# Weights times values in fp32 on two column tiles, and the gate function in three late ScalarE steps

## The chip, the core and the metric

The kernel runs on one core of a Trainium2 chip. The metric is device time in microseconds (us) of one execution, median of several. The engines are named as in the profile: PE (TensorE, matmul), PEld (its weight loads), DVE (VectorE), ACT (ScalarE), POOL (GpSimd), SP (SyncE, here only DMA issue).

## What is computed

A hybrid decoder trunk of two layers on x of 1024 rows by 1024 columns, all in float32. The first layer is differential attention (8 heads of two score maps each). From its output one shared K and V is projected. The second layer is stick-breaking attention with 16 heads of width 64. Each layer's mixer output is multiplied by a SiLU gate before the output projection and the residual add. The part that the change touches, from the reference:

```python
def _stick_breaking(q, k, v):
    ...
        z = jnp.einsum('bhqd,bshd->bhqs', qb, k).astype(jnp.float32) * scale
        log_beta = jax.nn.log_sigmoid(z)
        log_1mb = jnp.where(mask, jax.nn.log_sigmoid(-z), 0.0)
        suffix = lax.cumsum(log_1mb, axis=3, reverse=True) - log_1mb
        a = jnp.where(mask, jnp.exp(log_beta + suffix), 0.0)
        return jnp.einsum('bhqs,bshe->bhqe', a.astype(v.dtype), v)
...
    o = o.reshape(b, s, SB_W) * jax.nn.silu(g)
    return x + o @ w_out
```

## The kernel before

PE's fp32 work is mostly done as three products in a type of lower precision (fp32r): each operand is split into a high part (rounded) and a low part (the rest), and high*high, high*low and low*high are summed in PSUM. The high part is an ACT copy out of PSUM, the low part a DVE subtraction. So a projection block (`group`, lines 192 to 194) is 24 matmuls of 512 or 256 columns.

A layer (`run_layer`) works through head pairs. For the second layer a pair `p` has two heads `c` of 64 columns each. While the attention of one pair runs ("main"), the projections of the next pair (K, V, then Q and gate) are merged in between as "fill" by estimated costs (`merge`); after the last pair the fill is the output projection. The final order on each engine is set by a scheduler from those costs and from priorities: `hp()` raises the priority of what stands in it. Queues are in order: an instruction that waits holds up all behind it on its engine.

Attention of a pair goes over four groups `m` of 256 query rows, each in two steps `s_step` (128 rows, both heads) and then steps `t_step`:

- `s_step` (`unit_s_b`): scores on PE (line 235; the two heads use the upper and the lower 64 rows of the array), a copy of the scores from PSUM by ACT (line 778), a causal mask on POOL (line 780), then the stick-breaking chain: sign bit by DVE (787), Exp and Ln by ACT (788, 789), a min-and-subtract by DVE (790), a scan by DVE (792), Exp by ACT (793).
- `t_step(c, t)` (`unit_t_b`): one head `c` and 256 keys. `transposed` makes up to four 128x128 transposes on PE (line 263), the high part `th` by ACT (269) and the low part `tl` by DVE (270); the last step of a group leaves one block out and has it filled with zeros by POOL (267, 268). Then four fp32r matmuls of 256 columns (808, 809) add to PSUM tile `av`: the weights are a 128x128 tile that holds the high part of V in 64 columns and the low part in the other 64. At the end of a group ACT copies one half of `av` (814) and DVE adds the other (815).

A group `m` has `m`+1 such steps a head, so a pair has 20, and the layer has 160, with 640 matmuls of lines 808 and 809. The tiles of V are made by `v_done`: two ACT copies and two DVE subtractions for each half (752, 753).

The gate (`silu`, both layers, 16 calls each): ACT copies the projection from PSUM to `g` (210), DVE sets the sign bit (211), ACT does Exp and Ln (212, 213), DVE min-and-subtract (214), ACT Exp (215), POOL the product with `g` (216).

Of the kernel before, what the change touches and what calls it, by code (L numbers as in the profile page):

```python
# [24 lines left out]
HALF = 512  # L25
# [6 lines left out]
def f32(ap):  # L32
    return ap.bitcast(F32)


def build(tc, ins, out):
    nc = tc.nc
    act, dve, pool, pe = nc.scalar, nc.vector, nc.gpsimd, nc.tensor
# [4 lines left out]

    mk = lambda name, bufs, **kw: ctx.enter_context(tc.tile_pool(name=name, bufs=bufs, **kw))
    B = {"proj": 2, "sc": 2, "tr": 3, "av": 1, "th": 3, "g2k": 3, "o": 6, "w": 8, "raw": 3, "ta": 1, "g1k": 2, "hpr": 1, "small": 12, "qk": 2, "hpe": -1, "hpw": -1,
         "al": 6, "bl": 7, "tb": 3, "oa": 0, "la": 0, "lb": 8, "lt": 0, "lead": 1.0, "leada": 0.02, "leadb": 0.02, "leadxa": 0.15, "leadxb": 0.1, "holda": 0, "holdb": 0, "c2": 1, "gca": 0, "gcb": 0, "prea": 2, "preb": 1, "warm": 16, "wp": 2, "hpx": -1, "nx": 1, "nk": 6, "hpo": 0, "ob": 2}
# [8 lines left out]
    layer_pool = lctx.enter_context(tc.tile_pool(name="la", bufs=1))  # L55
    def hp(k="hpe"):
        return tc.high_priority(offset=None if B[k] < 0 else B[k])

    act.preload_act_table_set("natural_log_exp_and_others")

# [33 lines left out]
    ident = C("ident", [P, P])  # L94
# [10 lines left out]
    warm = PS("tr", B["tr"])  # L105
# [100 lines left out]
    def silu(pg, u):  # L206

        g = g2k()
        with hp():
            act.activation(g, pg, AF.Copy)  # L210
        dve.tensor_scalar(u.bitcast(I32), g.bitcast(I32), -0x80000000, None, ALU.bitwise_or)
        act.activation(u, u, AF.Exp)
        act.activation(u, u, AF.Ln, bias=1.0)
        dve.scalar_tensor_tensor(u, g, 0.0, u, ALU.min, ALU.subtract)
        act.activation(u, u, AF.Exp)
        pool.tensor_tensor(u, g, u, ALU.mult)

    def chunks(n):
        if n <= 512:
# [3 lines left out]
    HI = (slice(0, 64), slice(64, 128))  # L223
# [29 lines left out]
    def transposed(ae, ao, t, last):  # L253


        pt = PS("tr", B["tr"])
        order = (1, 0) if last else (0, 1)
        skip = P if last else 0
        for i, b in enumerate(order):
            for j, a in enumerate((ae, ao)):  # L260
                o = (i * 2 + j) * P
                if o >= skip:
                    pe.transpose(pt[:, o:o + P], a[:, (2 * t + b) * P:(2 * t + b + 1) * P], ident)  # L263
        th = T("th", [P, HALF], B["th"], F32R)
        tl = T("tl", [P, HALF], B["th"], F32R)
# [69 lines left out]

    def alloc_kv(hd):
        if hd.v is None:
            hd.v = [T("v", [P, 4, 2, P], 4, F32R) for _ in range(2)]
            hd.k = (T("kh", [P, S], 2, F32R), T("kl", [P, S], 2, F32R))

    def alloc_q(hd, hf):
# [355 lines left out]
    for j in range(2):  # L697
        g = gq16[:, j, :]
# [33 lines left out]
    def qkv_b(p):  # L732
        hd = heads_b[p]

        def q_done(hf, pt):
            with hp():
                split_q(alloc_q(hd, hf), pt, SCALE)

        def k_done(hf, pt):
            alloc_kv(hd)  # L740
            sl = slice(hf * HALF, (hf + 1) * HALF)
            with hp():
                split_k(hd.k, sl, pt, None)

        def v_done(hf, pt):
            tr = v_rows(pt)
            t3 = tr.rearrange("p (r j e) -> p r j e", r=4, j=2)
            for j in range(2):
                hi = hd.v[hf][:, :, j, 64 * j:64 * j + 64]
                lo = hd.v[hf][:, :, j, 64 - 64 * j:128 - 64 * j]  # L750
                with hp():
                    act.activation(hi, t3[:, :, j, :], AF.Copy)
                    dve.tensor_tensor(lo, t3[:, :, j, :], f32(hi), ALU.subtract)

        def proj(done):
            return lambda W, hf: proj_t(W, xT2, hf, lambda pt: done(hf, pt))

        return [(lambda: w_pair(w_kv[p], cols[:, 16:24]), [proj(k_done), proj(v_done)]),
                (lambda: w_pair(w_b[p], cols[:, 8:16]), [proj(q_done)])]

    def unit_s_b(p, m):
        hd = heads_b[p]

        def s_step(qb):
# [3 lines left out]
            n = (qb + 1) * P  # L768
# [6 lines left out]
            def evac(off, w, n, pt):  # L775
                for t, cs in zip(z, heads):
                    t3 = t[:, :w2].rearrange("p (c n) -> p c n", c=len(cs))
                    act.activation(t3[:, :, off:off + w], pt[:, cs[0]:cs[-1] + 1, :w], AF.Copy)  # L778
                    if off + w == n:
                        pool.affine_select(t3[:, :, n - P:], t3[:, :, n - P:], [[0, len(cs)], [-1, P]], ALU.is_ge, -BIG,  # L780
                                           base=-1, channel_multiplier=1)

            scores(hd.q[qb // 4], hd.k, qb, evac)
            for t in z:
                zc = t[:, :w2]
                u = u4k()[:, :w2]
# [11 lines left out]
    def unit_t_b(p, m):  # L798
        hd = heads_b[p]
        box = {}  # L800

        def t_step(c, t):
            if c == 0 and t == 0:
                box["p"] = PS("av", B["av"])
            pc = box["p"][:, c * 256:c * 256 + 256]
# [4 lines left out]
            if t == m:  # L810
                hi = slice(64 * c, 64 * c + 64)
                lo = slice(64 - 64 * c, 128 - 64 * c)
                oc = hd.o[m // 2][hi, (m % 2) * 256:(m % 2) * 256 + 256]
                act.activation(oc, pc[lo, :], AF.Copy)
                dve.tensor_tensor(oc, pc[hi, :], oc, ALU.add)
                if c == 1:
                    hd.done[m // 2] += 1

        return [(4 * 55 + 4 * 109, lambda c=c, t=t: t_step(c, t)) for c in range(2) for t in range(m + 1)]

    def sink_b(rb, t, cs):
        nc.sync.dma_start(out[0, rb * P:(rb + 1) * P, cs[0]:cs[1]], t[:, cs[0]:cs[1]])
# [56 lines left out]
```

## Time and profile before

| | us |
|---|---|
| median of 3 runs (1469.36 to 1471.21) | 1470.85 |
| the profiled execution | 1470.77 |
| its span (first to last instruction) | 1469.0 |
| PE busy in the span | 1414.9 |
| DVE busy | 1088.0 |
| ACT busy | 943.5 |
| POOL busy | 288.2 |

A matmul's time in the profile reaches from its start to the end of its results, and the next one begins earlier, so the price of a matmul in a stream is the distance between two starts, not its duration. In the table of stretches below, each row gives a stretch (from:to in us, then its length), and for each engine the busy time in it and the number of instructions, then the mean granted clock of PE (1.00 is 2.4 GHz; the other level, 1.2 GHz, counts 0.5). The first layer and its output projection reach to about 690 us; the attention of the second layer, from its first weights times values, to about 1410.

### The profile page before, as it was taken

The page shows a single profiled execution, that of the slowest core. Times are in us where ns is not written, and L with a number is a line of the kernel's source. Part 1 is how long each engine was busy: PE and PEld are TensorE (multiplying, and loading weights), DVE is VectorE, ACT ScalarE, POOL GpSimd, SP SyncE. Part 2 cuts the span into 40 slices and gives each one's busy share as a digit, 9 for nine tenths or more (in the row PEclk, how much of TensorE's full clock was granted, in tenths as well). Part 3 has the DMA queues.
Part 4 walks back from the last instruction along what each step waited for, and adds up shares of the span by engine and source line. Part 5 has one row for each costly group of instructions (what it writes and reads, how often), then busy time and mean ns, then how long its engine had stood idle before and what let it go on. Part 6 is the DMA issues. An engine that isn't in the chain of part 4 may idle for free.

```text
span 1469.0 us, 24503 instructions
## 1 busy us (share of the span) xinstructions
PE 1414.9 (96%) x8944; PEld 1192.0 (81%) x8944; DVE 1088.0 (74%) x2251; ACT 943.5 (64%) x1940; POOL 288.2 (20%) x545
## 2 busy tenths in 40 slices
PE   8999999999999999999999998998989999988899
PEld 7888888888888888799877776777867777767699
DVE  7586777777776867875458786887878788889952
ACT  7555566656565655453468777787777887788720
POOL 0111212121212112100011321322333242323100
PEclk9999999999999999999999998999999999998899
DMA  5111111111111124623111110111101010233412
GB/s 202 58 30 44 44 44 44 44 44 44 44 44 44 44 72 173 215 94 108 58 58 30 35 53 29 51 37 44 43 8 51 30 58 29 91 111 125 177 72 80
DMA packets 43113, 99.40 MB, mean 68 GB/s; under 512 B 4848, under 2 KB 6640, under 8 KB 41968
## 3 DMA queue, kind: packets, MB, share of 16 engines
q1 hardware_dynamic: 42992, 97.83, 19.4%
q8 instruction: 71, 1.16, 0.3%
q14 instruction: 50, 0.41, 0.1%
HBM read 74.74 MB, written 23.07 MB: 67 GB/s over the span
## 4 chain that ended last, share of the span: by engine, by line
PE 76%; DVE 12%; ACT 5%; issue 4%; DMA 1%; POOL 0%; SPq 0%; ACTq 0%; DVEq 0%; POOLq 0%
PE proj L192 18%; PE proj L193 18%; PE proj L194 17%; PE sc L235 8%; PE tr L263 5%; DVE u4k L792 5%; DVE u4k L790 2%; PE av L808 2%; PE av L809 2%; DVE tl L270 1%; PE av L638 1%; PE av L640 1%; PE av L639 1%; ACT u4k L788 1%; PE tr L571 1%
## 5 line engine op out<-in xcount | busy, mean ns | idle before, releaser
L192 PE MATMUL proj<-ah,w 128*128 128x512 f32 x768 | 310.3, 404 | 4.1 <-DVE kl L243 4.1
L193 PE MATMUL proj<-al,w 128*128 128x512 f32 x768 | 309.8, 403 | 0.0
L194 PE MATMUL proj<-ah,w 128*128 128x512 f32 x768 | 308.9, 402 | 0.0
L192 PE MATMUL proj<-w,ah 128*128 128x256 f32 x992 | 289.8, 292 | 4.0 <-DVE v L422 1.9
L194 PE MATMUL proj<-w,al 128*128 128x256 f32 x992 | 285.0, 287 | 0.0
L193 PE MATMUL proj<-w,ah 128*128 128x256 f32 x992 | 284.8, 287 | 0.0
L192 PEld LDWEIGHTS proj<-w,ah 128*128 128x128 f32 x992 | 191.3, 193 | 15.2 <-issue 5.8
L193 PEld LDWEIGHTS proj<-w,ah 128*128 128x128 f32 x992 | 191.5, 193 | 2.3 <-issue 1.0
L194 PEld LDWEIGHTS proj<-w,al 128*128 128x128 f32 x992 | 191.4, 193 | 1.5 <-issue 1.2
L192 PEld LDWEIGHTS proj<-ah,w 128*128 128x128 f32 x768 | 146.8, 191 | 39.8 <-DVE kl L243 5.6
L792 DVE TENSOR_TENSOR_SCAN u4k<-zl,u4k 128x768 f32<-128x768 f32 (+4 forms) x96 | 175.0, 1828 | 0.9
L193 PEld LDWEIGHTS proj<-al,w 128*128 128x128 f32 x768 | 146.9, 191 | 35.0 <-issue 7.1
L194 PEld LDWEIGHTS proj<-ah,w 128*128 128x128 f32 x768 | 146.5, 191 | 32.1 <-issue 3.0
L235 PE MATMUL sc<-kh,q 64*128 64x512 f32 (+2 forms) x768 | 159.7, 399 | 11.0 <-ACT zl L778 10.4
L270 DVE TENSOR_TENSOR tl<-tr,th 128x512 fp32r<-128x512 f32 (+1 forms) x240 | 146.5, 629 | 29.8 <-ACT th L269 28.6
L269 ACT ACTIVATE th<-tr 128x512 fp32r<-128x512 f32 (+1 forms) x240 | 126.2, 554 | 37.2 <-PE tr L263 32.1
L263 PE MATMUL tr<-ident,zl 128*128 128x128 f32 x864 | 131.0, 277 | 10.7 <-ACT zl L793 6.1
L793 ACT ACTIVATE zl<-u4k 128x768 f32<-128x768 f32 (+4 forms) x96 | 81.1, 846 | 87.9 <-DVE u4k L792 74.0
L161 ACT ACTIVATE w<-raw,cols 128x256 fp32r<-128x256 f32 x240 | 104.6, 502 | 46.6 <-PE proj L193 31.5
L780 POOL TENSOR_SCALAR_AFFINE_SELECT zl<-zl 128x128 f32<-128x128 f32 (+1 forms) x96 | 78.1, 819 | 278.9 <-ACT zl L778 278.7
L790 DVE SCALAR_TENSOR_TENSOR u4k<-zl,u4k 128x768 f32<-128x768 f32 (+4 forms) x96 | 95.5, 1007 | 44.9 <-ACT u4k L789 44.8
L235 PEld LDWEIGHTS sc<-kh,q 64*128 64x128 f32 x768 | 76.2, 186 | 62.7 <-issue 17.9
(148 smaller groups left out, 2630.7 us busy)
## 6 DMA issues: line engine op xcount, KB each, us to landing
raw<-in_w_kv_dram SPq DMA_DIRECT2D x32, 256.0 KB, 2.7
raw<-in_w_b_dram SPq DMA_DIRECT2D x32, 256.0 KB, 2.7
raw<-in_w_qk_dram SPq DMA_DIRECT2D x28, 256.0 KB, 2.7
raw<-in_w_vg_dram SPq DMA_DIRECT2D x28, 256.0 KB, 2.9
og_a<-o SPq DMA_DIRECT2D x28, 256.0 KB, 2.0
og_b<-o SPq DMA_DIRECT2D x28, 256.0 KB, 2.0
raw<-in_a_w_out_dram SPq DMA_DIRECT2D x26, 256.0 KB, 2.8
raw<-in_b_w_out_dram SPq DMA_DIRECT2D x26, 256.0 KB, 2.7
```

Of the source, the lines that this page charges most:

```text
L161: act.activation(h[:, i], r, AF.Copy, scale=g)
L192: pe.matmul(box["p"], lh, rh, start=(j == 0), stop=False)
L193: pe.matmul(box["p"], lh, rl, start=False, stop=False)
L194: pe.matmul(box["p"], ll, rh, start=False, stop=last)
L235: pe.matmul(pts[:, c, :wm], q[a][HI[c], rs_], k[b][HI[c], off:off + wm], start=(a + b == 0), stop=(a == 1))
L263: pe.transpose(pt[:, o:o + P], a[:, (2 * t + b) * P:(2 * t + b + 1) * P], ident)
L269: act.activation(th[:, skip:], pt[:, skip:], AF.Copy)
L270: dve.tensor_tensor(tl[:, skip:], pt[:, skip:], f32(th[:, skip:]), ALU.subtract)
L780: pool.affine_select(t3[:, :, n - P:], t3[:, :, n - P:], [[0, len(cs)], [-1, P]], ALU.is_ge, -BIG, base=-1, channel_multiplier=1)
L790: dve.scalar_tensor_tensor(u, zc, 0.0, u, ALU.min, ALU.subtract)
L792: dve.tensor_tensor_scan(ur, t[:, 1:w2 + 1][:, ::-1], ur, 0.0, ALU.add, ALU.subtract)
L793: act.activation(zc, u, AF.Exp, scale=-1.0)
```

## The change

In the second layer alone, a `t_step` now takes both heads. Each head's transposed block is copied once to a fp32 tile `tt` (head 0 by ACT, head 1 by DVE), with no low part and no zero block. V is one fp32 tile a pair, written by one ACT copy for each half. The matmuls take fp32 operands: weights of 128 keys by 64 columns, one head to output partitions 0 to 63 and the other to 64 to 127, that is two column tiles of the array. A group ends in one DVE copy of `av`. The first layer's `th` and `tl` move to its own pool of tiles.

In both layers the gate is now: DVE copies the projection from PSUM with a lower bound of -80, and ACT does Exp(-g), Ln(1+u) and Exp(-u), and POOL the product; what follows the DVE copy has a lowered priority (`later`, offset -400). The copy of the scores from PSUM gets a raised priority.

```diff
+    def later():
+        return tc.high_priority(offset=-B["late"])
...
         with hp():
-            act.activation(g, pg, AF.Copy)
-        dve.tensor_scalar(u.bitcast(I32), g.bitcast(I32), -0x80000000, None, ALU.bitwise_or)
-        act.activation(u, u, AF.Exp)
-        act.activation(u, u, AF.Ln, bias=1.0)
-        dve.scalar_tensor_tensor(u, g, 0.0, u, ALU.min, ALU.subtract)
-        act.activation(u, u, AF.Exp)
-        pool.tensor_tensor(u, g, u, ALU.mult)
+            dve.tensor_scalar(g, pg, -80.0, None, ALU.max)
+        with later():
+            act.activation(u, g, AF.Exp, scale=-1.0)
+            act.activation(u, u, AF.Ln, bias=1.0)
+            act.activation(u, u, AF.Exp, scale=-1.0)
+            pool.tensor_tensor(u, g, u, ALU.mult)
...
-            for j in range(2):
-                hi = hd.v[hf][:, :, j, 64 * j:64 * j + 64]
-                lo = hd.v[hf][:, :, j, 64 - 64 * j:128 - 64 * j]
-                with hp():
-                    act.activation(hi, t3[:, :, j, :], AF.Copy)
-                    dve.tensor_tensor(lo, t3[:, :, j, :], f32(hi), ALU.subtract)
+            with hp():
+                act.activation(hd.v[hf].rearrange("p r e -> p (r e)"), tr, AF.Copy)
...
-                    act.activation(t3[:, :, off:off + w], pt[:, cs[0]:cs[-1] + 1, :w], AF.Copy)
+                    with hp():
+                        act.activation(t3[:, :, off:off + w], pt[:, cs[0]:cs[-1] + 1, :w], AF.Copy)
...
-        def t_step(c, t):
...
-            for i, (kb, th, tl) in enumerate(transposed(hd.at[2 * m][c], hd.at[2 * m + 1][c], t, t == m)):
-                vt = hd.v[kb // 4][:, kb % 4, c, :]
-                pe.matmul(pc, vt, th, start=(t + i == 0), stop=False)
-                pe.matmul(pc, vt, tl, start=False, stop=(t + i == m + 1))
...
+        def t_step(t):
...
+            for c in range(2):
...
+                for i, (a, b) in enumerate(((ae, 0), (ao, 0), (ao, 1), (ae, 1))[:n // P]):
+                    pe.transpose(pt[:, i * P:(i + 1) * P], a[:, (2 * t + b) * P:(2 * t + b + 1) * P], ident)
+                tt = T("tt", [P, HALF], 4, pool=layer[0])
+                if c == 0:
+                    act.activation(tt[:, :n], pt[:, :n], AF.Copy)
+                else:
+                    dve.tensor_copy(tt[:, :n], pt[:, :n])
+                at.append(tt)
+            for c in range(2):
+                vt = hd.v[t // 2][:, 2 * (t % 2), HI[c]]
+                pe.matmul(po[HI[c], :], vt, at[c][:, 0:256], start=(t == 0), stop=False)
+            for c in range(2):
+                vt = hd.v[t // 2][:, 2 * (t % 2) + 1, HI[c]]
+                if last:
+                    pe.matmul(po[HI[c], P:256], vt, at[c][:, 256:384], start=False, stop=True)
+                else:
+                    pe.matmul(po[HI[c], P:256], vt, at[c][:, 256:384], start=False, stop=False)
+                    pe.matmul(po[HI[c], 0:P], vt, at[c][:, 384:512], start=False, stop=False)
+            if last:
+                oc = hd.o[m // 2][:, (m % 2) * 256:(m % 2) * 256 + 256]
+                dve.tensor_copy(oc, po)
```

The order of the instructions on PE before, at weights times values of the first pair's second group (`av` is the accumulator, `th` and `tl` the parts of the transposed weights, `v` the tile of V, `tr` a transposed block, `proj` a projection):

```order
L808 MATMUL av_9578<-th_9584,v_8964 128x256
L192 MATMUL proj_9893<-ah_8656,w_9217 128x512
L193 MATMUL proj_9893<-al_8657,w_9217 128x512
L809 MATMUL av_9578<-tl_9585,v_8964 128x256
L808 MATMUL av_9578<-th_9584,v_8964 128x256
L809 MATMUL av_9578<-tl_9585,v_8964 128x256
L808 MATMUL av_9578<-th_9597,v_8964 128x256
L809 MATMUL av_9578<-tl_9598,v_8964 128x256
L808 MATMUL av_9578<-th_9597,v_8964 128x256
L809 MATMUL av_9578<-tl_9598,v_8964 128x256
L808 MATMUL av_9578<-th_9651,v_8965 128x256
```

The same place with the change, two steps of that pair (`tt_9513` and `tt_9574` are head 0's, `tt_9520` and `tt_9581` head 1's), and a little later a third, where scores (`sc`) stand between:

```order
L825 MATMUL av_9507<-tt_9520,v_8932 64x256
L831 MATMUL av_9507<-tt_9513,v_8932 64x128
L832 MATMUL av_9507<-tt_9513,v_8932 64x128
L831 MATMUL av_9507<-tt_9520,v_8932 64x128
L832 MATMUL av_9507<-tt_9520,v_8932 64x128
L825 MATMUL av_9507<-tt_9574,v_8932 64x256
L825 MATMUL av_9507<-tt_9581,v_8932 64x256
L831 MATMUL av_9507<-tt_9574,v_8932 64x128
L832 MATMUL av_9507<-tt_9574,v_8932 64x128
L831 MATMUL av_9507<-tt_9581,v_8932 64x128
L832 MATMUL av_9507<-tt_9581,v_8932 64x128
```

```order
L237 MATMUL sc_9703<-kh_8933,q_1663_9116 128x384
L825 MATMUL av_9507<-tt_9617,v_8932 64x256
L831 MATMUL av_9507<-tt_9610,v_8932 64x128
L832 MATMUL av_9507<-tt_9610,v_8932 64x128
L831 MATMUL av_9507<-tt_9617,v_8932 64x128
L832 MATMUL av_9507<-tt_9617,v_8932 64x128
L825 MATMUL av_9507<-tt_9642,v_8932 64x256
L237 MATMUL sc_9703<-kh_8933,q_1663_9116 128x384
```

What moved: one head's products before stand together and alternate between high and low part; now the heads take turns, all products of a head's second key block in a row, and the first product of head 0 often stands by itself, ahead of others (its partner waits for the DVE copy).

DVE at the same place, before (`u4k` is the stick-breaking chain's tile):

```order
L787 TENSOR_SCALAR u4k_9548<-zl_9535 128x512
L270 TENSOR_TENSOR tl_9585<-tr_9579,th_9584 128x512
L270 TENSOR_TENSOR tl_9598<-tr_9592,th_9597 128x512
L270 TENSOR_TENSOR tl_9652<-tr_9646,th_9651 128x512
L790 SCALAR_TENSOR_TENSOR u4k_9548<-zl_9535,u4k_9548 128x512
L792 SCALAR_TENSOR_TENSOR u4k_9548<-zl_9535,u4k_9548 128x512
L270 TENSOR_TENSOR tl_9680<-tr_9675,th_9679 128x384
L270 TENSOR_TENSOR tl_9697<-tr_9691,th_9696 128x512
L270 TENSOR_TENSOR tl_9723<-tr_9717,th_9722 128x512
```

and with the change (the copies of head 1, and between them the gate's copy, line 213):

```order
L792 SCALAR_TENSOR_TENSOR u4k_9480<-zl_9467,u4k_9480 128x512
L794 SCALAR_TENSOR_TENSOR u4k_9480<-zl_9467,u4k_9480 128x512
L821 COPY tt_9520<-tr_9515 128x512
L821 COPY tt_9581<-tr_9576 128x512
L213 TENSOR_SCALAR g2k_9739<-proj_9671 128x512
L821 COPY tt_9617<-tr_9612 128x512
L821 COPY tt_9648<-tr_9644 128x384
```

What moved: the subtractions, one for each head and step, have become half as many copies, and they now stand behind the scan of the chain instead of around it; the gate's copy out of PSUM stands on DVE among them.

## Rows read from the trace of the kernel before

**Rows 1.** The page: busy time and share of the span of each engine.

```profile
PE 1414.9 (96%) x8944; PEld 1192.0 (81%) x8944; DVE 1088.0 (74%) x2251; ACT 943.5 (64%) x1940; POOL 288.2 (20%) x545
```

**Rows 2.** Busy time by stretch of 100 us: PE, PEld, DVE, ACT, POOL, granted clock.

```profile
200.00:300.00 100.00, 100.00 (x707) 86.94 (x706) 75.67 (x215) 64.72 (x157) 17.77 (x31) 1.00 0.15 49
800.00:900.00 100.00, 100.00 (x550) 79.50 (x551) 76.87 (x115) 75.27 (x143) 23.57 (x54) 1.00 0.13 43
900.00:1000.00 100.00, 88.19 (x465) 68.51 (x464) 79.59 (x111) 78.02 (x145) 25.37 (x58) 0.92 0.10 33
1000.00:1100.00 100.00, 95.25 (x523) 74.33 (x522) 81.50 (x109) 77.35 (x140) 28.24 (x55) 0.96 0.10 32
1100.00:1200.00 100.00, 96.54 (x515) 75.69 (x514) 84.94 (x117) 78.22 (x144) 35.94 (x56) 0.98 0.14 48
1200.00:1300.00 100.00, 96.31 (x535) 76.53 (x533) 84.79 (x112) 76.95 (x138) 29.53 (x55) 0.97 0.20 70
1300.00:1400.00 100.00, 82.72 (x556) 70.76 (x555) 92.17 (x131) 78.63 (x139) 26.13 (x62) 0.90 0.37 132
```

**Rows 3.** Waits of PE from 690 to 1410 us: total us, times, longest.

```profile
PE sc L235 <- ACT zl L778: 10.4, 9, 2.7
PE av L809 <- DVE tl L270: 7.0, 9, 2.8
```

**Rows 4.** Timeline of PE at 1121 us: start, us, instruction, count.

```profile
1120.74 0.28 PE L808 MATMUL av<-th,v 128*128 128x256 f32 x1
1120.86 0.33 PE L809 MATMUL av<-tl,v 128*128 128x256 f32 x1
...
1122.79 0.28 PE L235 MATMUL sc<-kl,q 64*128 64x256 f32 x2
1122.90 0.28 PE L235 MATMUL sc<-kh,q 64*128 64x256 f32 x2
1123.11 0.50 PE L192 MATMUL proj<-ah,w 128*128 128x512 f32 x1
```

**Rows 5.** Timeline of PE at 307 us, the first layer's fp32 product.

```profile
307.19 0.60 PE L645 MATMUL tr<-t1k,ones 128*128 128x256 f32 x2
307.63 1.03 PE L571 MATMUL tr<-ident,qk 128*128 128x128 f32 x8
```

**Rows 6.** Groups from 690 to 1410 us: count | busy us, mean ns | idle before.

```profile
L270 DVE TENSOR_TENSOR tl<-tr,th 128x512 fp32r<-128x512 f32 (+1 forms) x160 | 96.0, 627 | 15.6 <-ACT th L269 14.4
L815 DVE TENSOR_TENSOR o<-av,o 64x256 f32<-64x256 f32 x63 | 26.3, 417 | 15.6 <-ACT o L814 14.7
L753 DVE TENSOR_TENSOR v<-tr,v 128x256 fp32r<-128x256 f32 x32 | 13.3, 416 | 11.0 <-ACT v L752 10.9
L214 DVE SCALAR_TENSOR_TENSOR o<-g2k,o 128x512 f32<-128x512 f32 x16 | 11.6, 728 | 5.1 <-ACT o L213 5.1
L211 DVE TENSOR_SCALAR o<-g2k 128x512 int32<-128x512 int32 x16 | 6.5, 418 | 4.8 <-ACT g2k L210 4.8
L357 DVE CAST o<-o 128x512 fp32r<-128x512 f32 x14 | 6.2, 446 | 1.6 <-POOL o L356 1.6
L269 ACT ACTIVATE th<-tr 128x512 fp32r<-128x512 f32 (+1 forms) x160 | 82.4, 555 | 6.8 <-PE av L808 3.6 <-PE tr L263 2.1
L814 ACT ACTIVATE o<-av 64x256 f32<-64x256 f32 x63 | 23.8, 379 | 18.0 <-PE av L809 16.8
L210 ACT ACTIVATE g2k<-proj 128x512 f32<-128x512 f32 x16 | 9.5, 592 | 4.9 <-PE proj L194 4.9
```

**Rows 7.** Line 808 by stretch: where the weights times values lie.

```profile
690.00:900.00 210.00, 15.65 (x58) 10.96 (x58) 1.00 0.17 55
900.00:1300.00 400.00, 53.75 (x191) 37.00 (x190) 0.96 0.13 46
1300.00:1400.00 100.00, 17.57 (x59) 12.42 (x59) 0.90 0.37 132
```

**Rows 8.** DVE's line 270 in the last stretch, 1300 to 1400 us.

```profile
L270 DVE TENSOR_TENSOR tl<-tr,th 128x512 fp32r<-128x512 f32 (+1 forms) x30 | 18.3, 626 | 0.4 <-ACT th L269 0.2
```

More of the change, by code (lines that the diff above doesn't have):

```diff
@@ L45, in build @@
     B = {"proj": 2, "sc": 2, "tr": 3, "av": 1, "th": 3, "g2k": 3, "o": 6, "w": 8, "raw": 3, "ta": 1, "g1k": 2, "hpr": 1, "small": 12, "qk": 2, "hpe": -1, "hpw": -1,
-         "al": 6, "bl": 7, "tb": 3, "oa": 0, "la": 0, "lb": 8, "lt": 0, "lead": 1.0, "leada": 0.02, "leadb": 0.02, "leadxa": 0.15, "leadxb": 0.1, "holda": 0, "holdb": 0, "c2": 1, "gca": 0, "gcb": 0, "prea": 2, "preb": 1, "warm": 16, "wp": 2, "hpx": -1, "nx": 1, "nk": 6, "hpo": 0, "ob": 2}
+         "al": 6, "bl": 7, "tb": 3, "oa": 0, "la": 0, "lb": 8, "lt": 0, "lead": 1.0, "leada": 0.02, "leadb": 0.02, "leadxa": 0.15, "leadxb": 0.1, "holda": 0, "holdb": 0, "c2": 1, "gca": 0, "gcb": 0, "prea": 2, "preb": 1, "warm": 16, "wp": 2, "hpx": -1, "nx": 1, "nk": 6, "hpo": 0, "ob": 2, "late": 400}
     ORDERS = ((0, 1, 2, 3), (3, 0, 2, 1), (1, 3, 0, 2), (2, 0, 3, 1), (3, 2, 1, 0), (1, 2, 0, 3), (0, 2, 1, 3), (2, 3, 0, 1),
@@ L263, in transposed @@
                     pe.transpose(pt[:, o:o + P], a[:, (2 * t + b) * P:(2 * t + b + 1) * P], ident)
-        th = T("th", [P, HALF], B["th"], F32R)
-        tl = T("tl", [P, HALF], B["th"], F32R)
+        th = T("th", [P, HALF], B["th"], F32R, layer[0])
+        tl = T("tl", [P, HALF], B["th"], F32R, layer[0])
         if last:
@@ L337, in alloc_kv @@
         if hd.v is None:
-            hd.v = [T("v", [P, 4, 2, P], 4, F32R) for _ in range(2)]
+            if layer[1]:
+                v = T("v", [P, 8, P], 4)
+                hd.v = [v[:, 0:4], v[:, 4:8]]
+            else:
+                hd.v = [T("v", [P, 4, 2, P], 4, F32R) for _ in range(2)]
             hd.k = (T("kh", [P, S], 2, F32R), T("kl", [P, S], 2, F32R))
@@ L746, in v_done @@
             tr = v_rows(pt)
-            t3 = tr.rearrange("p (r j e) -> p r j e", r=4, j=2)
-            for j in range(2):
-                hi = hd.v[hf][:, :, j, 64 * j:64 * j + 64]
-                lo = hd.v[hf][:, :, j, 64 - 64 * j:128 - 64 * j]
-                with hp():
-                    act.activation(hi, t3[:, :, j, :], AF.Copy)
-                    dve.tensor_tensor(lo, t3[:, :, j, :], f32(hi), ALU.subtract)
+            with hp():
+                act.activation(hd.v[hf].rearrange("p r e -> p (r e)"), tr, AF.Copy)
         def proj(done):
@@ L800, in unit_t_b @@
         box = {}
-        def t_step(c, t):
-            if c == 0 and t == 0:
+        def t_step(t):
+            if t == 0:
                 box["p"] = PS("av", B["av"])
-            pc = box["p"][:, c * 256:c * 256 + 256]
-            for i, (kb, th, tl) in enumerate(transposed(hd.at[2 * m][c], hd.at[2 * m + 1][c], t, t == m)):
-                vt = hd.v[kb // 4][:, kb % 4, c, :]
-                pe.matmul(pc, vt, th, start=(t + i == 0), stop=False)
-                pe.matmul(pc, vt, tl, start=False, stop=(t + i == m + 1))
[L810 to L817, printed above, removed]
@@ L819, in unit_t_b @@
-        return [(4 * 55 + 4 * 109, lambda c=c, t=t: t_step(c, t)) for c in range(2) for t in range(m + 1)]
+            po = box["p"][:, :256]
+            last = t == m
+            at = []
+            for c in range(2):
+                ae, ao = hd.at[2 * m][c], hd.at[2 * m + 1][c]
+                pt = PS("tr", B["tr"])
+                n = HALF - P if last else HALF
+                for i, (a, b) in enumerate(((ae, 0), (ao, 0), (ao, 1), (ae, 1))[:n // P]):
[6 more added lines that the diff above has]
+                at.append(tt)
@@ new lines, in t_step @@
+            for c in range(2):
[5 more added lines that the diff above has]
+                    pe.matmul(po[HI[c], P:256], vt, at[c][:, 256:384], start=False, stop=True)
+                else:
+                    pe.matmul(po[HI[c], P:256], vt, at[c][:, 256:384], start=False, stop=False)
+                    pe.matmul(po[HI[c], 0:P], vt, at[c][:, 384:512], start=False, stop=False)
@@ L821, in sink_b @@
+            if last:
+                oc = hd.o[m // 2][:, (m % 2) * 256:(m % 2) * 256 + 256]
+                dve.tensor_copy(oc, po)
+                hd.done[m // 2] += 1
+        return [(8 * 55 + 4 * 109 * 2, lambda t=t: t_step(t)) for t in range(m + 1)]
     def sink_b(rb, t, cs):
```

## The prediction

> **What bounds the kernel now.** The page comes first: PE is busy 96% of the span, DVE 74%, ACT 64% [rows 1]. That is a mean over unlike stretches, so the table of stretches is read next [rows 2]. From 200 to 300 and from 800 to 900 us PE has no idle time at all, at a DVE share of 75.67 and 76.87 and an ACT share of 64.72 and 75.27. From 900 us on DVE rises to 80 to 92, ACT to 77 to 79, and PE idles: 11.8, 4.8, 3.5 and 3.7 us in the four stretches to 1300, together 23.7, and 17.3 in the last. In the same five stretches, the ones in which PE idled, the granted clock falls to 0.92, 0.96, 0.98, 0.97 and 0.90. The two levels are 1.0 (2.4 GHz) and 0.5 (1.2 GHz), so each hundredth that is missing is 1 us of PE work lost in 100: 8 + 4 + 2 + 3 = 17 us, and 10 in the last. So 40.7 us can be won back from 900 to 1300, and 27.3 from 1300 to 1400. The waits of PE name the causes: the score copy of ACT, 10.4 us, and DVE's low part before weights times values, 7.0 us [rows 3].
>
> The kernel is thus bound by PE to 900 us and by PE together with late DVE and ACT work behind it. The change relieves DVE and ACT and loads PE; the question is which is more.
>
> **What PE gets.** Before, 640 matmuls of lines 808 and 809, whose starts lie 0.12 us apart in a stream [rows 4], are 76.8 us. With the change the operands are fp32. The one fp32 product before is line 645: two instructions of 256 columns, and the next one starts 0.44 us after them [rows 5], so 0.22 us a pass of 256 columns and 0.11 of 128, two passes a product. The layer has 80 steps of two heads. In 48 of them stand two products of 256 columns and four of 128, 2 x 0.44 + 4 x 0.22 = 1.76 us one after another; in the 32 that end a group two and two, 1.32 us. In a row that is 84.5 + 42.2 = **126.7 us**.
>
> No column tiles stand in the trace. The nearest rows are the scores, on two row tiles: two matmuls of 256 columns end in the 0.28 us of one, and the next pair starts 0.11 us later [rows 4]. I take column tiles to run side by side in the same way. The upper bound is the 126.7 above, the lower half of it, 63.4. Between them lies the order. Instructions of PE start in order, and the two passes of a product need the same tile. So head 1's first pass starts together with head 0's second; its second pass runs beside the first two 128-column passes of head 0; the two that follow of head 0 hold up head 1 until the last of them starts. That is 0.22 x 3 + 0.11 x 5 = 1.21 us for a full step and 0.88 for a last one: 58.1 + 28.2 = 86.2 us. In the listing of the changed order I count 29 places where head 0's first product stands by itself; each loses one pass of overlap, 29 x 0.22 = 6.4. That makes 92.6 us.
>
> A change of tiling has a price as well: after the last pair of scores the projection starts 0.21 us later and not 0.11 [rows 4], so 0.10. The listing has 102 runs of column-tile products between other work, two changes each: 20.4 us. Sum: 113.0 us in place of 76.8, **+36 us of PE work**, 126.7 + 20.4 = 147.1 at worst (+70) and 63.4 + 20.4 = 83.8 at best (+7).
>
> The Trainium skill (TensorEngine Tiling (Array Packing), Tiling Modes, Key Properties) speaks against the change here: a change of tiling mode drains TensorE. A full drain would be the 0.28 us of a matmul less the 0.12 in which the next normally starts, 0.16 a change, and 102 x 2 x 0.06 = 12 us more than my sum; the row of the scores shows 0.10, and I stay with it.
>
> Line 808 lies with 58 of its 308 instructions from 690 to 900 us, 191 from 900 to 1300, 59 after that [rows 7]. The +36 thus fall as +6.8, +22.3 and +6.9.
>
> **What DVE and ACT lose.** From DVE go lines 270, 815, 753, 214 and 211: 96.0 + 26.3 + 13.3 + 11.6 + 6.5 = 153.7 us in the second layer [rows 6]. Added: 80 copies from PSUM, between 0.446 (a copy that isn't from PSUM, line 357) and 0.627 (line 270, two operands); I take 0.60, as ACT's copy of 512 columns (line 210, 0.592) is near it: 48 us. Then 32 copies of the accumulator at no more than line 815's 0.417, 13 us, and 16 copies of the gate at 0.60, 10 us. DVE has **83 us less**. ACT loses half of line 269 (41), line 814 (24), line 210 (9.5) and some 3 of V: **77 us less**. Four fifths of the steps lie from 900 to 1400 us, which is 13 points less DVE and 12 less ACT: DVE at 67 to 72 and ACT at 65 from 900 to 1300. That is below the load at which PE had no idle time [rows 2].
>
> - From 690 to 900 us nothing idles, so PE's work is paid in full: **+6.8**.
> - From 900 to 1300 us I take nine tenths of the 40.7 as won (the waits end, and with them the half clock), -36.6, and +22.3 paid: **-14.3**.
> - From 1300 to 1400 us DVE is busy 92 of 100, mostly with the chain's own scans, which stay. Line 270 has 30 instructions there, 18.3 us [rows 8], and line 815 its share, 4.9. In their place come 15 copies at 0.60 and 6 at 0.417: 12 us less. PE's work there, 73 + 6.9 = 80, fits. I take **-9**, the rest goes to gaps of the chain.
>
> **What I put at nothing.** The gate in the first layer: DVE trades 0.418 + 0.728 for 0.60, ACT loses a copy, and PE, at 100, covers it. The late gate keeps a buffer of `g` (three in all, shared with V's rows) until POOL's product; if it were kept too long, the copy of the next gate or V projection would wait, and PE for its PSUM tile. The listing has the ACT steps some twenty rows behind at most, so I count 0; uncovered it costs three ACT steps of about 0.6 us a gate. The raised score copy attacks the 10.4 us [rows 3], which are in the 40.7. A step now needs both heads' copies, and the projections stand behind a waiting product on PE; that wait is the 7.0 of line 809 in a new form, now behind one copy and not a copy and a subtraction. POOL's zero blocks go; nobody waited for POOL.
>
> Sum: 6.8 - 14.3 - 9 = -16.5 us against the profiled execution's 1470.77 (its span of 1469.0 and 1.8 around it; the median is 1470.85, the same): **1454 us**.
>
> **Rivals.**
> - *Column tiles one after another.* PE +70, that is +13.2, +43.6, +13.5. Then 13.2 + 43.6 - 36.6 = +20, and the last stretch gives 6: +14, **1485 us**, slower. For it: no row shows column tiles, and fp32 on them is unseen; against it, the scores. It decides from about 56 us of added PE work (0.81 x 56 = 36.6 + 9).
> - *Full overlap.* PE +7: 1.3 + 4.3 - 36.6 - 11 = -42, **1429 us**. For it: half the work is in each tile; against it, two passes of one head stand together in the order.
> - *The waits stay.* They come from the length of the stick-breaking chain, not from load. Then of the 40.7 only three tenths go: 6.8 + 22.3 - 12 - 4 = +13, **1484 us**. For it: the chain has six steps between DVE and ACT, each queued; against it, 800 to 900 us, the same chain with no idle PE.
> - *It moves nothing that counts*: 1468 to 1474 us.
>
> The Trainium skill (TensorE: Matmul & The Clock Gate, Part 3, Measured speedup vs the span model) gives 2.38 for three column tiles; as an estimate for two, 1.59, that would be 126.7 / 1.59 = 80 us before changes of tiling, nearer my 92.6 than either bound. No run here shows it yet.
>
> **Chances.** Forecast 0.50, one after another 0.22, full overlap 0.12, the waits stay 0.12, nothing 0.04. A difference of 0.2% (3 us) is about what a measurement can tell from none. Faster: nearly all of the forecast, full overlap and little of the two slow cases, 0.64; same 0.07; slower 0.29. The range leaves out half of the full overlap's spread below and the upper part of the slow cases: 1428 to 1488. The forecast's own range, by the copy's and the switch's bounds, is 1440 to 1466.
>
> **What would show it.** Starts of the two heads' products a few ns apart or one pass apart (overlap), or 0.44 (none); idle PE and granted clock from 900 to 1300 near 0 and 1.00; DVE near 70 there; the copies near 0.60; gaps of 0.10 at each change of tiling. I am wrong if the av products take over 133 us, or if PE still idles 20 us or more from 900 to 1300.

## The result: 1484 us, slower, and the profile after

The changed kernel takes **1484.08 us** (median of 4 runs, 1483.53 to 1486.47) against 1470.59 beside it: ratio 1.0096, 95% interval [1.0078, 1.0113]. The forecast was 1454; 1484 lies in the range, on the side that I gave 0.29.

The page's busy line of the changed kernel, to be read beside [rows 1]:

```profile
PE 1429.1 (96%) x9136; PEld 1167.0 (79%) x9136; DVE 1010.8 (68%) x2075; ACT 869.1 (59%) x1748; POOL 275.6 (19%) x417
```

Over the whole program DVE lost 77 us and ACT 74. My 83 and 77 were for the second layer alone; from 690 us on DVE lost 67 (588.6 to 521.7) and ACT 64 (539.7 to 475.6). PE idles for 1484.7 - 1429.1 = 55.6 us of its span, before 54.1: nothing was won there. The stretches, columns as in [rows 2]:

```profile
800.00:900.00 100.00, 100.00 (x587) 74.66 (x586) 68.86 (x92) 64.03 (x115) 25.48 (x36) 1.00 0.13 43
900.00:1000.00 100.00, 89.11 (x506) 64.66 (x504) 64.25 (x83) 63.96 (x113) 26.18 (x37) 0.93 0.10 32
1000.00:1100.00 100.00, 87.47 (x473) 64.04 (x473) 71.49 (x86) 63.94 (x108) 30.82 (x35) 0.88 0.11 38
1100.00:1200.00 100.00, 95.99 (x550) 68.66 (x549) 71.50 (x89) 69.15 (x120) 21.46 (x37) 0.98 0.11 38
1200.00:1300.00 100.00, 97.93 (x554) 70.80 (x554) 70.77 (x88) 69.93 (x113) 28.08 (x36) 0.98 0.16 54
1300.00:1400.00 100.00, 88.95 (x594) 69.25 (x593) 74.06 (x99) 56.15 (x97) 21.40 (x34) 0.93 0.37 132
```

DVE is at 64 to 72 and ACT at 64 to 70 from 900 to 1300 us, the load that I had forecast, and still PE idles 10.9 + 12.5 + 4.0 + 2.1 = 29.5 us there (before 23.7), and the granted clock gives away 7 + 12 + 2 + 2 = 23 us (before 17). So less load on DVE and ACT did not end PE's waits. They are, from 690 to 1425 us, against [rows 3]:

```profile
PE sc L237 <- ACT zl L780: 14.4, 8, 2.8
PE proj L195 <- DVE kl L245: 14.3, 5, 4.0
PE tr L816 <- ACT zl L795: 7.6, 4, 3.4
```

Two waits of before that [rows 3] leaves out belong beside the last two, a transpose's for `zl` and a projection's for `kl`:

```profile
PE tr L263 <- ACT zl L793: 6.1, 7, 2.3
PE proj L192 <- DVE kl L243: 4.1, 3, 3.0
```

The wait for the low part is gone; that for the score copy has grown from 10.4 to 14.4, and that of a projection for `kl`, a DVE subtraction of the next pair's K, from 4.1 to 14.3. In three head pairs they lie close together, at 910, 999 and 1085 us; in two more, at 1178 and 1260, the wait for `kl` stands without the other. The timeline around the first such place, all engines, with the idle time before and its releaser in brackets:

```profile
905.29 0.42 DVE L835 COPY o<-av 128x256 f32<-128x256 f32 x1 [4.78 <-PE av L829]
906.16 0.32 POOL L774 MEMSET zl<- 128x1 f32 x2 [5.96 <-issue]
...
910.10 0.50 PE L237 MATMUL sc<-kh,q 64*128 64x512 f32 x2 [1.77 <-ACT zl L780]
...
913.82 0.69 PE L237 MATMUL sc<-kh,q 64*128 64x384 f32 x2 [2.76 <-ACT zl L780]
913.89 3.98 DVE L794 TENSOR_TENSOR_SCAN u4k<-zl,u4k 128x640 f32<-128x640 f32 x2
...
918.25 1.28 DVE L245 TENSOR_TENSOR kl<-proj,kh 128x512 fp32r<-128x512 f32 x2
918.98 0.80 PE L195 MATMUL proj<-ah,w 128*128 128x512 f32 x1 [3.83 <-DVE kl L245]
```

A group of weights times values ends (905.29), the next score tiles `z` (`zl` in the rows) get their first write right after (906.16, with no wait for a tile named before it), and then PE has three score groups in its queue one behind another, each waiting for the copies of the one before; the projection behind them waits for `kl`, which stands behind two scans on DVE. In short stretches around it, columns as in [rows 2]:

```profile
908.00:914.00 6.00, 1.47 (x14) 0.79 (x14) 4.50 (x5) 5.77 (x12) 5.31 (x5) 0.78 0.23 86
914.00:920.00 6.00, 2.17 (x8) 1.48 (x9) 5.99 (x6) 2.21 (x3) 2.53 (x2) 0.50 0.00 1
920.00:926.00 6.00, 6.00 (x19) 4.67 (x18) 4.30 (x5) 4.45 (x6) 0.48 (x1) 0.58 0.01 3
```

PE idles 4.53 + 3.83 = 8.4 of 12 us, and the clock is at its lower level from 914 to 920 and for most of the 6 us after, when PE is busy again: that is the second price of a stall, 2.5 us in this stretch.

The column tiles do overlap. PE's timeline at 1022 us shows twelve instructions between two lots of transposes. They are as many as a full step has, but by the order listed ahead of the prediction they belong to two. Head 0's first product stands alone before the transposes, at 1021.19; then come head 1's first product and both heads' later ones, and last head 0's first product of the next step:

```profile
1022.46 0.43 PE L825 MATMUL av<-tt,v 128*64 128x256 f32 x1
1022.47 0.43 PE L831 MATMUL av<-tt,v 128*64 128x128 f32 x2
1022.73 0.38 PE L825 MATMUL av<-tt,v 128*64 128x256 f32 x1
1022.74 0.38 PE L832 MATMUL av<-tt,v 128*64 128x128 f32 x2
1022.95 0.27 PE L831 MATMUL av<-tt,v 128*64 128x128 f32 x1
1022.96 0.42 PE L825 MATMUL av<-tt,v 128*64 128x256 f32 x1
1023.06 0.27 PE L831 MATMUL av<-tt,v 128*64 128x128 f32 x1
1023.16 0.27 PE L832 MATMUL av<-tt,v 128*64 128x128 f32 x1
1023.22 0.38 PE L825 MATMUL av<-tt,v 128*64 128x256 f32 x1
1023.27 0.27 PE L832 MATMUL av<-tt,v 128*64 128x128 f32 x1
1023.53 0.76 PE L816 MATMUL tr<-ident,zl 128*128 128x128 f32 x5
```

Starts of the two heads lie 0.01 us apart (1022.46 and 1022.47, 1022.73 and 1022.74, 1022.95 and 1022.96), and the twelve take 1023.53 - 1022.46 = 1.07 us, with the second of the two changes of tiling in it. The same passes are 1.76 us without overlap and 0.88 with full overlap; I had 1.21 for a step, in another order, and 0.10 a change.

The copies, groups from 690 to 1425 us, columns as in [rows 6]:

```profile
L821 DVE COPY tt<-tr 128x512 f32<-128x512 f32 (+1 forms) x77 | 48.3, 630 | 54.8 <-PE tr L816 54.7
L819 ACT ACTIVATE tt<-tr 128x512 f32<-128x512 f32 (+1 forms) x77 | 41.8, 548 | 19.5 <-PE tr L816 17.2 <-PE av L832 2.1
L835 DVE COPY o<-av 128x256 f32<-128x256 f32 x30 | 12.6, 420 | 26.2 <-PE av L829 25.9
L213 DVE TENSOR_SCALAR g2k<-proj 128x512 f32<-128x512 f32 x16 | 10.8, 676 | 6.5 <-PE proj L197 6.5
```

### The profile page after: what moved, and what is told of

It reads as the page before. It is cut to its first block, busy times and chain, and to the rows that moved or that the text cites. A ratio compares the mean times of both kernels' runs of the same rounds, so it can differ in the third digit from the quotient of the medians.

```text
span 1484.7 us, 24193 instructions
## 1 busy us (share of the span) xinstructions
PE 1429.1 (96%) x9136; PEld 1167.0 (79%) x9136; DVE 1010.8 (68%) x2075; ACT 869.1 (59%) x1748; POOL 275.6 (19%) x417
## 4 chain that ended last, share of the span: by engine, by line
PE 91%; DVE 3%; issue 2%; ACT 2%; DMA 1%; POOL 1%; SPq 0%; POOLq 0%; DVEq 0%; ACTq 0%
PE proj L195 21%; PE proj L196 20%; PE proj L197 20%; PE sc L237 9%; PE tr L816 5%; PE av L825 4%; PE tr L265 2%; PE av L646 1%; PE av L644 1%; PE av L645 1%; PE tr L281 1%; PE tr L651 1%; PE tr L577 1%; PE tr L136 1%; PE av L832 1%
## 5 line engine op out<-in xcount | busy, mean ns | idle before, releaser
L195 PE MATMUL proj<-ah,w 128*128 128x512 f32 x768 | 312.4, 407 | 14.3 <-DVE kl L245 14.3
L237 PE MATMUL sc<-kh,q 64*128 64x512 f32 (+2 forms) x768 | 159.8, 403 | 17.0 <-ACT zl L780 14.4
L782 POOL TENSOR_SCALAR_AFFINE_SELECT zl<-zl 128x128 f32<-128x128 f32 (+1 forms) x96 | 90.6, 949 | 343.2 <-ACT zl L780 342.2
L165 DVE SCALAR_TENSOR_TENSOR w<-raw,cols,w 128x256 fp32r<-128x256 f32 x240 | 108.5, 502 | 30.4 <-ACT w L164 29.2
L615 DVE CUSTOM_DVE_ANT_0 zl<-sc,mask_a 128x384 f32<-128x384 f32 (+3 forms) x192 | 99.0, 552 | 40.5 <-PE sc L237 40.4
L780 ACT ACTIVATE zl<-sc 128x512 f32<-128x512 f32 (+4 forms) x160 | 82.8, 549 | 66.9 <-PE sc L237 42.8
```

What stands on the lines that cost most here:

```text
L165: dve.scalar_tensor_tensor(l[:, i], r, g, f32(h[:, i]), ALU.mult, ALU.subtract)
L195: pe.matmul(box["p"], lh, rh, start=(j == 0), stop=False)
L237: pe.matmul(pts[:, c, :wm], q[a][HI[c], rs_], k[b][HI[c], off:off + wm], start=(a + b == 0), stop=(a == 1))
L615: dve.tensor_tensor_reduce(p[c][:, off:off + w], pts[:, c, :w], mask, 1.0, BIG, ALU.add, ALU.min, mn[c][:, k:k + 1])
```

## The experiments

All ratios are to the kernel before, run on the same chip in the same job, with 95% intervals.

### The change taken in halves

**Weights times values alone** (fp32 column tiles and the new V; gate and score copy as before).

```diff
-            dve.tensor_scalar(g, pg, -80.0, None, ALU.max)
-        with later():
...
+            act.activation(g, pg, AF.Copy)
+        dve.tensor_scalar(u.bitcast(I32), g.bitcast(I32), -0x80000000, None, ALU.bitwise_or)
...
-                    with hp():
-                        act.activation(t3[:, :, off:off + w], ...)
+                    act.activation(t3[:, :, off:off + w], ...)
```

> Only the weights times values in fp32 on two column tiles, with the V tiles; gate and score copy as before. Theory B (pair boundary: the stall of PE where one head pair ends stays or grows because the weights times values no longer stand there as filler, whatever the DVE and ACT load): 1480 to 1488 us, and from 900 to 1300 us still 25 us or more of idle PE. Rival G (the gate copy on DVE or the raised score copy makes the loss, the fp32 products alone gain): 1450 to 1466 us.

1479.81 us, 1.0061 [1.0046, 1.0076]: this half alone is slower.

**Gate and score copy alone** (against the kernel before).

```diff
-            act.activation(g, pg, AF.Copy)
-        dve.tensor_scalar(u.bitcast(I32), g.bitcast(I32), -0x80000000, None, ALU.bitwise_or)
...
+            dve.tensor_scalar(g, pg, -80.0, None, ALU.max)
+        with later():
...
-                    act.activation(t3[:, :, off:off + w], ...)
+                    with hp():
+                        act.activation(t3[:, :, off:off + w], ...)
```

> Only the gate in three late steps with its copy on DVE, and the raised score copy; weights times values as before. Theory B: 1464 to 1474 us, about the kernel before. Rival G: 1480 us or more.

1459.01 us, 0.9922 [0.9908, 0.9937]. PE's longest waits from 690 to 1425 us are still those for the score copy (before 10.4) and for the low part (before 7.0):

```profile
PE sc L237 <- ACT zl L781: 9.5, 6, 4.1
PE av L812 <- DVE tl L272: 7.6, 12, 1.8
PE av L811 <- DVE o L818: 5.4, 5, 1.9
PE proj L195 <- DVE kl L245: 4.7, 4, 2.3
```

So 12 us are won by the gate and the raised copy, and lost again when the other half is there: 1484 together, 1480 without them. The waits do not show where they are won; over the span PE idles 1458.4 - 1409.2 = 49.2 us, before 54.1, and the granted clock is 0.985, before 0.980.

### Details of the change, and other buffers

**Score copy at usual priority.**

```diff
-                    with hp():
-                        act.activation(t3[:, :, off:off + w], ...)
+                    act.activation(t3[:, :, off:off + w], ...)
```

> The changed kernel with the score copy at its usual priority again. Theory B: 1480 to 1490 us. Rival G, in the form that the raised score copy pushes the copies of K behind it: 1465 us or less.

1485.11, 1.0097 [1.0082, 1.0112]. **Gate steps at usual priority.**

```diff
-        with later():
+        with ExitStack():
```

> The changed kernel with the gate's ACT and POOL steps at their usual priority (the copy stays on DVE). Theory B: 1480 to 1490 us. Rival G, in the form that late gate steps of ACT crowd the boundary of the pairs: 1470 us or less.

1486.07, 1.0099 [1.0082, 1.0116]. Neither moves the changed kernel: what costs is in the other half.

**A third pair of K buffers** (every third pair uses a spare tile of V's size for `kh` and a new tile for `kl`), against the wait for `kl`.

```diff
-            hd.k = (T("kh", [P, S], 2, F32R), T("kl", [P, S], 2, F32R))
+            n_k[0] += layer[1]
+            if n_k[0] and n_k[0] % 3 == 0:
+                hd.k = (T("v", [P, S], 4, F32R), T("klx", [P, S], 1, F32R, layer[0]))
+            else:
+                hd.k = (T("kh", [P, S], 2, F32R), T("kl", [P, S], 2, F32R))
```

> The changed kernel with a third pair of K buffers in turn, so that the next but one pair's K can leave PSUM before the last scores of the running pair. Theory K (both projection PSUM tiles are held by K at the pair boundary until its buffer is free, and PE has no projection to do): 1468 to 1476 us, with the waits of projections for the low part of K nearly gone. Theory Z (the scores come late because tiles of z are freed late, by the joint steps of both heads): 1480 to 1486 us.

1477.78, 1.0055 [1.0038, 1.0071]. The wait for `kl` falls from 14.3 us to 3.2, that for the score copy only from 14.4 to 11.9, and 6 of the 14 us to be explained go. So the K tiles are a part at most.

**Three PSUM tiles for projections, two for transposes**, against the place in PSUM.

```diff
-    B = {"proj": 2, "sc": 2, "tr": 3, ...
+    B = {"proj": 3, "sc": 2, "tr": 2, ...
```

> The changed kernel with three PSUM tiles for projections and two for transposes. Theory K: 1470 to 1478 us, PE has one more projection to do at the boundary. Theory Z: 1482 us or more, the transposes get later and free z later.

1559.63, 1.0613 [1.0598, 1.0629]: far worse; it has a transpose tile less, a cost that can hide what it was to show, so I take nothing from it on the cause.

**The second key block's products of the two heads in turn**, in place of head 0's and then head 1's.

```diff
-            for c in range(2):
...
-                if last:
...
+            for i in range(1 if last else 2):
+                for c in range(2):
+                    vt = hd.v[t // 2][:, 2 * (t % 2) + 1, HI[c]]
+                    cols_ = slice(0, P) if i else slice(P, 256)
+                    pe.matmul(po[HI[c], cols_], vt, at[c][:, 256 + i * P:384 + i * P], start=False, stop=last)
```

> The changed kernel with the second key block's products of the two heads in turn (head 0, head 1, head 0, head 1) and not two and two. If starts in order cost overlap as the prediction had it, 48 steps win one half pass pair each, about 5 us: 1478 to 1481 us. If the reordering by the hardware or the boundary hides it: 1483 to 1486 us.

1479.59, 1.0065 [1.005, 1.008].

### The score tiles z

What the joint step changed beside PE's work: a `t_step` reads the tiles `z` of both heads, so all of a group's tiles stay held to its last step; before, head 0's came free when its steps were done (in rows over 512 keys, where each head has a tile of its own). There are seven.

**An eighth z**, in the changed kernel and in weights times values alone.

```diff
-         "al": 6, "bl": 7, ...
+         "al": 6, "bl": 8, ...
```

> The changed kernel with eight tiles of z and not seven. Theory Z: 1462 to 1474 us, and POOL's first write of z waits much less for the transposes (93.6 us in the changed kernel, 44.5 before). Theory K: 1480 to 1486 us.

> The fp32 products on column tiles alone (gate and score copy as before) with eight tiles of z. Theory Z: 1442 to 1456 us, some 30 us under the same with seven tiles (1479.8), so the loss of the products alone was the tiles too. If the gate and the score copy are what eight tiles set free: 1470 us or more.

**1440.04 us, 0.9795 [0.9781, 0.981]**, and 1443.09, 0.9817 [0.9801, 0.9833]. One tile turns the change from 0.96% slower to 2.05% faster. Busy line and stretches of the first:

```profile
PE 1416.6 (99%) x9136; PEld 1152.5 (80%) x9136; DVE 1006.3 (70%) x2075; ACT 867.8 (60%) x1748; POOL 257.7 (18%) x417
...
900.00:1000.00 100.00, 98.99 (x553) 70.86 (x551) 74.53 (x89) 68.47 (x116) 25.63 (x36) 1.00 0.12 43
1000.00:1100.00 100.00, 98.61 (x569) 70.59 (x569) 74.36 (x95) 72.24 (x125) 23.18 (x40) 1.00 0.13 46
1100.00:1200.00 100.00, 99.24 (x567) 72.66 (x565) 73.92 (x92) 67.83 (x115) 22.08 (x35) 1.00 0.10 35
1200.00:1300.00 100.00, 99.76 (x604) 71.60 (x603) 72.14 (x92) 71.09 (x124) 27.31 (x42) 1.00 0.25 91
1300.00:1400.00 100.00, 95.16 (x724) 78.62 (x723) 79.26 (x112) 56.56 (x90) 17.96 (x26) 1.00 0.38 132
```

From 900 to 1300 PE idles 3.4 us and the clock is full: of the 40.7 us [rows 2] 37 are won, with DVE at 72 to 75 and ACT at 68 to 72, if anything above the load that I had forecast.

**The kernel before with eight z.** For room, `th` and `tl` have two tiles in place of three in the second layer, so a control has that and seven z.

```diff
-         "al": 6, "bl": 7, ...
+         "al": 6, "bl": 8, ...
...
-        th = T("th", [P, HALF], B["th"], F32R)
-        tl = T("tl", [P, HALF], B["th"], F32R)
+        th = T("th", [P, HALF], B["th"] - layer[1], F32R, layer[0])
+        tl = T("tl", [P, HALF], B["th"] - layer[1], F32R, layer[0])
```

> The kernel before with eight tiles of z; for the room the second layer has two and not three of the high and low transposed weights. Theory Z in its strict form (the joint steps make the tiles short, the old order did not): within 10 us of the next kernel. If seven tiles were too few before as well: 15 us or more under the next kernel.

> The kernel before with seven tiles of z and two of the high and low transposed weights in the second layer: the control of the kernel with eight. 1470 to 1490 us; the difference of the two is the price of the eighth tile before the change.

1466.73, 0.9982 [0.9969, 0.9995], and 1477.1, 1.0047 [1.003, 1.0064]. There the eighth tile is worth 10 us, in the changed kernel four times as much, 44 (37 for weights times values alone). That the joint steps are the reason does not follow from this pair alone: in the kernel before with eight, PE's longest waits are for the low part (15.0 and 11.5 us), which no score tile shortens. Gate and raised copy with the old steps and eight `z`, or fp32 column tiles with a step for each head, would tell; neither was run.

**Six z** in the changed kernel: the miss.

> The changed kernel with six tiles of z and not seven. Theory Z (the joint steps of both heads hold z longer, and seven tiles bind): at least 30 us slower than the changed kernel, 1515 us or more. If eight tiles helped by a lucky order of the queues alone: within 10 us of 1484.

1469.76, 1.0002 [0.9992, 1.0011]: with a tile less it was faster by 14 us, where I had expected it slower by 30 or more. Four more runs were made on what the number does: five, six with the score copy at usual priority, nine (here `tt` has three tiles in place of four, for room), and the kernel before with six.

```diff
-         "al": 6, "bl": 7, ...
+         "al": 6, "bl": 9, ...
...
-                tt = T("tt", [P, HALF], 4, pool=layer[0])
+                tt = T("tt", [P, HALF], 3, pool=layer[0])
```

> The changed kernel with five score tiles. By the shortage alone, each tile less costs, and five lie over 1500. If the pairing of tiles decides, five (odd) are worse than six and at least 1484. If the times at six and seven are only chance of the order, five can lie anywhere, 1465 to 1520.

> Six score tiles without the raised score copy: another order of the same work. With seven tiles four other orders gave 1478 to 1486 (with it or without it the same). If six tiles are better than seven by their number, this stays at 1465 to 1475; if the 1470 of six was luck of one order, it goes to 1480 or more.

> The changed kernel with nine score tiles z (and three copies tt in place of four, to make room). Seven tiles gave 1484, eight 1440, six 1470. If a shortage of z is the whole cause and eight are enough, nine give 1436 to 1446 and PE idles under 25 us. If odd numbers are bad because a step over more than 512 keys takes two tiles and one is left over, nine lie clearly above eight, 1450 to 1485. If three tt are too few, PE's waits for the copies (L819, L821) grow by over 5 us.

> The kernel before with six score tiles in place of seven. In it a group's two heads follow one another, so that two of a large group's four tiles come free halfway; by that reading its threshold lies at six (four and two) and below the changed kernel's eight (four and four): 1465 to 1482. If the number of tiles as such decides, not how long the steps hold them, it loses at six what the changed kernel loses from eight to seven (44 us) or more: 1505 and above.

Five: 1526.34, 1.0371 [1.0347, 1.0395]. Six in another order (score copy not raised): 1482.84, 1.0076 [1.0052, 1.01]. Nine: 1437.23, 0.9763 [0.9737, 0.979]. Before with six: 1480.05, 1.0067 [1.0049, 1.0085]. Two stretches with five, and then the same two with nine:

```profile
1000.00:1100.00 100.00, 89.61 (x500) 63.09 (x499) 61.07 (x83) 65.75 (x118) 20.89 (x41) 0.96 0.10 32
1100.00:1200.00 100.00, 91.56 (x485) 64.64 (x482) 66.20 (x86) 64.00 (x108) 19.63 (x33) 0.92 0.11 38
```

```profile
1000.00:1100.00 100.00, 100.00 (x574) 71.26 (x573) 77.76 (x95) 70.40 (x123) 29.12 (x40) 1.00 0.14 45
1100.00:1200.00 100.00, 100.00 (x585) 72.70 (x585) 75.09 (x97) 72.57 (x125) 25.12 (x36) 1.00 0.11 36
```

| z tiles | 5 | 6 | 7 | 8 | 9 |
|---|---|---|---|---|---|
| changed kernel, us | 1526 | 1470 and 1483 | 1478 to 1486, five kernels | 1440 and 1439 | 1437 (three `tt`) |
| kernel before, us | | 1480 | 1471 | 1467 (two `th`) | |

In the changed kernel the number decides: a step between five and six, none between six and seven beyond what another order of the same work does (13 us at six), a step at eight, none after. No order crosses that step: the six kernels with fp32 column tiles and seven `z` take 1478 to 1486 (leaving out the one with two transpose tiles), the four with eight or nine 1437 to 1443. I read the 1470 of six tiles as one lucky order, for which two orders are thin evidence. The code gives a count that fits, though no run shows it by itself. A row over more than 512 keys takes two tiles, so groups 2 and 3 take four and groups 0 and 1 two; the pair's order is 1, 3, 0, 2, and a group's steps stand after the next group's scores. When group 2 begins, group 3's four and group 0's two can still be held, and its first row needs two: 4 + 2 + 2 = 8. Six or seven both leave that row waiting for the end of group 3, since one free tile is no use to a row that takes two; five do not hold group 3 and group 0. Before, two of group 3's four are free halfway, so by this count six are enough; with six that kernel loses 9 us, where the changed one loses 44 from eight to seven.

How the shortage reaches PE stays open. POOL's first write of a tile waits for transposes of the old content 215.2, 138.4, 93.6, 84.1 and 43.6 us in all with five, six, seven, eight and nine tiles (six in the order that takes 1470); that does not go with the times, which fall by 44 us from seven to eight and hardly from eight to nine. What the traces do show is another order on PE: with seven tiles, three score groups stand side by side at 908 us, and with eight the groups of the same sizes stand apart, with other work between them:

```profile
893.40 0.39 PE L237 MATMUL sc<-kh,q 64*128 64x256 f32 x2
900.26 0.50 PE L237 MATMUL sc<-kh,q 64*128 64x512 f32 x2
907.87 0.44 PE L237 MATMUL sc<-kh,q 64*128 64x384 f32 x2
```

But three side by side stand in the changed kernel only at 908, 996 and 1083 us, and nowhere in weights times values alone (1480) or without the raised score copy (1485), which have seven tiles too and are as slow. So this is one form that the loss takes, not the cause of it in all orders.

**Eight z, and the heads' products in turn**: is PE's work the bound once there are tiles enough? The edits are the two above (`"bl": 8`, and the loop over `i` outside that over `c`).

> Eight score tiles, and the second key block's products of the two heads in turn, so that head 1's passes are held up less: by the count of passes 0.88 us in place of 1.21 for a full step less one pass, 48 steps, about 5 us less PE work at best. With seven tiles the same edit gave 4.5 us (1479.6 against 1484.1), but PE stood idle there. If PE's work is now the bound, 1434 to 1437; if the heads' starts already interleave, 1440.

1438.51, 0.9774 [0.9752, 0.9797], against 0.9795 [0.9781, 0.981]: no difference that the intervals show, and the time lies between the two that I had expected, so this edit does not decide. That PE is the bound is read from the busy line above: 99% with eight tiles.

## Why the prediction was wrong

**The step that failed** is "from 900 to 1300 us I take nine tenths of the 40.7 as won". Its ground was load: DVE and ACT would fall below the load at which PE had no idle time from 800 to 900 us [rows 2]. They did fall below it, and nothing was won: idle and lost clock went from 40.7 to 52.5 us. What I did not ask is how long a step now holds its inputs. I followed the new copies, the accumulator and the buffer of `g`, and noted that a step "now needs both heads' copies", but not that its `z` tiles come free later, with seven of them. With eight the step holds as it stands: 37 of 40.7. That one tile more is what was missing is shown; that it was missing because the joint step holds its tiles longer is argued from the code. I had also named two waits of PE as the causes and passed over the one for `kl` (4.1 us), which grew to 14.3.

**The rival "the waits stay" gave the time (1484) by luck, with the wrong cause.** It put them down to the length of the stick-breaking chain; with the chain as it is, eight tiles end most of them.

**PE's price was too high.** The column tiles run side by side, so the rival "one after another" falls, and my term held in kind: I summed over the 102 runs of products the distance from the end of the slot of the matmul before to the start of the one after: 105.5 us, where I had 113.0 (109.3 in the 110 runs of the kernel with eight z). What I compared it with was a bare stream of 76.8; by the same measure the 142 runs of before take 119.9 with their waits, and 95.7 with each run at the median of its length. By medians the eight-z kernel's runs are 106.1, so the products cost 10 us more than before, and 29 at most against the bare stream, not 36. A second reading gives more than 10: with eight tiles PE is busy 1416.6 us at a mean granted clock of 0.998, before 1414.9 at 0.980, which is, as an estimate, up to 0.018 x 1469 + 1.7 = 28 us more work. Cheaper products are one reason why eight z end at 1440 and not at 1454. The last stretch is another: I took 9 there, and with eight tiles idle time and lost clock from 1300 to 1400 us fall from 27.3 to 4.8. How the 14 us divide is not shown.

The premise of my count, that starts follow the order of the products, did not hold: at 1022 us both passes of head 0's product start (1022.47, two of them) before the second pass of head 1's, which by the listing stands ahead of it (1022.73). The Trainium skill (TensorEngine Tiling (Array Packing), Tiling Modes, Key Properties) has a change of mode drain the engine. A lone product, two instructions, took 0.67 us in 29 places where 0.44 is its bare time, and there up to 0.11 a change is left: near my 0.10, and less than the 0.16 that I had estimated for a full drain.

**How much overlaps.** The twelve instructions at 1022 us give 1.76 / 1.07 = 1.64. The Trainium skill (TensorE: Matmul & The Clock Gate, Part 3, Measured speedup vs the span model) had led me to an estimate of 1.59 for two column tiles, and the trace agrees.

**DVE and ACT**: 67 and 64 us less from 690 us on, forecast 83 and 77 for the second layer. The DVE lines that I had summed lose 153.7 - 80 x 0.630 - 32 x 0.420 - 16 x 0.676 = 79, so the sum held and other lines took longer. The copies take 0.63 and not 0.60 on average, the gate's 0.676 and not 0.60, the accumulator's 0.420 (0.417).

**From 1300 to 1400 us** PE idles 11.1 us (before 17.3), with the clock at 0.93 and not 0.90, so some of the 9 us came; with eight tiles it idles 4.8 at full clock. **Put at nothing**: the late gate cost nothing in its place (1486 without it). That gate and raised copy by themselves gain 12 us I had not counted apart from the 40.7; a raised copy in the changed kernel gains nothing (1485 without it).

Of my two signs of being wrong, the products' 133 us did not come, the 20 us of idle PE did (29.5).

## What to carry to other kernels

When a change joins two steps that ran one after the other, list each buffer that the joint step reads, and count anew how many must be alive at the worst place of the order, for the rows that take two; here the count gives 8 where 7 were there, and one tile less turned a gain of 2% into a loss of 1%. Falling load on the engines behind the bound does not end its waits if those come from buffers, and a run with one buffer more tells it at once. Such a count wants several values and orders: another order moved the time by 13 us at the same number, and the one point at six would have led away from the cause.

## What the runs showed of the hardware

- Two fp32 products on two column tiles start 0.01 us apart, as the scores on row tiles do, and twelve instructions, as many as a step has, take 1.07 us from the first start to the next matmul's, where the same passes one after another are 1.76. The second pass of a product can start after both passes of the product behind it in the order, on the other tile (1022.73, after the two from 1022.47).
- A DVE copy of 512 columns from PSUM to an fp32 tile is no cheaper than the two-operand subtraction it replaces: 0.630 on average with its shorter form, against 0.627 [rows 6].
- A stall of 8.4 us cost 2.5 us more in the following 6, in which PE was busy at a granted clock of 0.58. With nine tiles, where PE has no idle time from 1000 to 1200 us, the clock stays at 1.00.
